# Side steps of a hybrid decoder trunk: a pause ahead of three-matrix groups, additions one step at a time at a shorter period, and one product for the values of the first 128 keys

## The chip, the cores and the metric

The kernel runs on one core of one Trainium2 chip. The metric is the device time of that core in microseconds, the median of three runs. The core has a matrix engine (PE, with its weight loads shown as PEld), a vector engine (DVE), a scalar engine (ACT), a general engine (POOL) that here mostly issues transfers, and a queue (SP) that issues the other transfers. Each engine and each queue runs its own instructions in a fixed order and waits where one of them needs something that is not there yet.

## The reference

A trunk of two layers over 256 positions of width 2048, in 32-bit floats:

```python
for layer in range(DEPTH):                      # DEPTH = 2
    mix = even_mixer(h, ...) if layer % 2 == 0 else odd_mixer(h, ...)
    h = layer_norm(ALPHA * h + mix, ...)
    h = layer_norm(ALPHA * h + conv_ffn(h, ...), ...)

def conv_ffn(x, w_up, conv_w, conv_b, w_down):
    a, u = jnp.split(x @ w_up, 2, axis=-1)      # 2048 -> 2 x 5632
    a = causal_depthwise_conv(a, conv_w, conv_b)
    return (jax.nn.silu(a) * u) @ w_down        # 5632 -> 2048
```

The even mixer holds a state-space scan (16 heads) and a softmax attention (8 heads); the odd mixer holds an attention with three branches (compressed keys, selected keys, window; 8 heads) and a retention (8 heads). At 256 positions every key is in reach, so an attention head is causal attention over two tiles of 128 keys: the first 128 queries see the first 128 keys, the second 128 queries see all 256.

## The kernel before

**Numbers in two parts.** A 32-bit product is made of three products of shorter numbers: ACT rounds a block of weights to its high part (`whi`, line 210), DVE subtracts to get the low part (`wlo`, line 218), and PE multiplies high by high, low by high and high by low. A block (a slab) is 128 x 1024 numbers, 512 KB. SP loads slabs into six buffers `wraw`; there are four buffers each of `whi` and `wlo`. `Weights.get(i)` (line 258) prepares slabs up to `i + 3` before the products of slab `i` are written down.

**Ordinary groups.** `group_b` (387) computes 256 columns over 16 tiles of 128 rows: 4 slabs of 4 tiles, products in line 427. With its last tile it writes the evacuation of the group (`ev_a` with the convolution, lines 1667 to 1684, or `ev_u`, 1686 to 1694), which runs on ACT and DVE. After every second tile it takes one step from each of two queues of side work, `self.fill` and `self.aux`. So such a group has eight places for a step; the last one stands behind the evacuation. The first group of an up phase, of three column blocks, has 15 places.

**Wide groups and kept sums.** `group_m` (517) computes 1024 columns and saves products in some pairs of row tiles: seven small products of sums of blocks replace eight. Plans name pairs: `P` plain, `N` with weight sums made on the spot by DVE (`add_up`, 224, four additions into the tile `other` or `sums`), `R` with weight sums made earlier and kept in memory. Up phases hold wide groups at j = 7 in layer 0 and at j = 4, 8 and 12 in layer 1 (`WIDE_UP`, line 36), all with the plan `NPNPNPNP`. A wide group of an up phase takes its side steps from `aux` alone (line 525: `fill = self.aux if inner else self.fill`); `self.fill` stands still in it.

**Side work of an up phase.** `Weights.make` (231) gives three steps for a kept sum: `load` (POOL brings four blocks into `sums`, two transfers of 512 KB, line 240), `add` (DVE, four additions of 128 x 512 in one step, line 246, each depending on the one before) and `store` (POOL writes the result back, two transfers, line 250). All of them are pinned: they stay behind whatever was written earlier for their engine. `cycles` (483) lays these steps into `self.fill` with empty steps between them, `period` steps for a sum. With one buffer the next load cannot start until the store has landed. Layer 0 makes six sums with two buffers at period 10 and then 15 with one at period 13; layer 1 makes 15 with one buffer at period 14 (`CYCLES`, line 38). The even layer makes two at period 20. Behind each wide group six empty steps are put at the head of `self.fill` (line 1725).

`residual` (863) lays its steps into `aux`: four loads of two rows into the tile `room` (POOL, line 869, pinned), and behind each of them two pairs of vector instructions, `gain` (873, pinned) and `bias` (877). The POOL queue thus carries loads and stores of sums and these row loads in the order of the steps.

**Other places.** `sum_up` (499) makes sums of activations for the pairs with seven products: five vector instructions and a split. `attn_steps` (1086) gives three steps for a head; the last, `mix` (1148), multiplies the softmax weights by the values, in full 32-bit products: three in the even layer, eight in the odd one, all 128 columns wide.

Instructions are ordered within an engine by a planner that keeps pinned ones in place and otherwise takes what it believes ready first.

## Time and profile before

| what | value |
|---|---|
| median of three runs | 2248.83 us (2248.74 to 2249.03) |
| span of the profiled execution | 2246.8 us |
| PE busy | 2235.3 us, 99% of the span |
| PEld busy | 1920.9 us, 85% |
| DVE busy | 1831.3 us, 82% |
| ACT busy | 1254.0 us, 56% |
| POOL busy | 126.4 us, 6% |
| mean granted clock | 0.999 |
| transfers | 546.33 MB, 243 GB/s in the mean |

The page gives the span of the profiled execution, from its first to its last instruction, and no other time for it; the median of the runs is 2.03 us above that span, which is what lies around it. A row of a timeline gives start, length, engine, line, operation, what is written from what, shape, the number of instructions merged into the row, and in brackets the idle time before it with what ended it. A matmul's length is modelled, and successive ones overlap; the distance from start to start is what one costs. A product of full 32-bit numbers shows as two records.

### The profile page before, as it was taken

What the parts mean: (1) busy time and instruction counts of PE and PEld (TensorE: products, weight loads), DVE (VectorE), ACT (ScalarE), POOL (GpSimd) and SP (SyncE); (2) the same over time, 40 slices, a digit from 0 to 9 for tenths busy, and PEclk for the clock granted to TensorE, in tenths of its full rate; (3) what the DMA queues carried; (4) which work ended last, traced back from release to release, by engine and by line L of the source; (5) the groups of instructions that cost most, each with busy time, mean ns of one, the idle gap of its engine ahead of it and who ended that gap; (6) DMA issues with size and microseconds to landing.
All of it is one profiled execution on the core that took longest, in us unless ns stands there. A gap on an engine that the chain in (4) does not pass through costs nothing.

```text
span 2246.8 us, 32995 instructions
## 1 busy us (share of the span) xinstructions
PE 2235.3 (99%) x12125; PEld 1920.9 (85%) x12125; DVE 1831.3 (82%) x2795; ACT 1254.0 (56%) x1718; POOL 126.4 (6%) x219
## 2 busy tenths in 40 slices
PE   9999999999999999999999999999999999999998
PEld 9888888888888888888898888888888888888887
DVE  5788688988877778887977777889988887779887
ACT  5555555655555556656645564457555565557563
POOL 0101000110011100000000000000100001100000
PEclk9999999999999999999999999999999999999999
DMA  9854456897788886888668534467876768888884
GB/s 312 292 175 161 158 194 189 274 376 264 238 302 302 296 284 213 292 286 274 211 208 287 188 114 154 152 209 235 290 227 228 255 217 297 300 273 276 276 280 169
DMA packets 158780, 546.33 MB, mean 243 GB/s; under 512 B 17827, under 2 KB 19283, under 8 KB 158483
## 3 DMA queue, kind: packets, MB, share of 16 engines
q1 hardware_dynamic: 132937, 451.41, 60.1%
q0 software_dynamic: 25536, 92.55, 11.8%
q8 instruction: 95, 1.56, 0.3%
q14 instruction: 68, 0.56, 0.1%
q10 hardware_dynamic: 144, 0.26, 0.0%
HBM read 502.19 MB, written 41.96 MB: 242 GB/s over the span
## 4 chain that ended last, share of the span: by engine, by line
PE 96%; DVE 2%; issue 1%; ACT 0%; POOL 0%; DMA 0%; SPq 0%; ACTq 0%; POOLq 0%; DVEq 0%
PE acc L427 51%; PE ps L540 7%; PE ps L541 7%; PE ps L539 7%; PE acc L627 3%; PE acc L629 3%; PE acc L628 3%; PE acc L540 3%; PE acc L541 3%; PE acc L539 3%; PE ps L628 1%; PE ps L627 1%; PE ps L629 1%; PE ps L1161 1%; PE ps L427 1%
## 5 line engine op out<-in xcount | busy, mean ns | idle before, releaser
L210 ACT ACTIVATE whi<-wraw 128x1024 fp32r<-128x1024 f32 (+4 forms) x882 | 875.1, 1002 | 549.6 <-PE acc L427 219.0
L218 DVE TENSOR_TENSOR wlo<-wraw,whi 128x1024 fp32r<-128x1024 f32 (+4 forms) x882 | 1007.5, 1153 | 209.6 <-ACT whi L210 197.6
L427 PE MATMUL acc<-x,whi 128*128 128x512 f32 x3296 | 1032.2, 398 | 0.0
L427 PEld LDWEIGHTS acc<-x,wlo 128*128 128x128 f32 x3296 | 604.0, 188 | 136.5 <-DVE wlo L218 0.3
L427 PE MATMUL acc<-x,wlo 128*128 128x256 f32 x3296 | 633.8, 279 | 0.0
L427 PEld LDWEIGHTS acc<-x,whi 128*128 128x128 f32 x3296 | 510.0, 189 | 9.7 <-issue 1.1
L689 ACT ACTIVATE tmp<-acc 128x512 f32<-128x512 f32 x104 | 62.2, 598 | 167.8 <-PE acc L427 167.7
L246 DVE TENSOR_TENSOR sums<-sums 128x512 f32<-128x512 f32 x140 | 96.2, 687 | 10.5 <-DMA sums<-in_down 9.4
L540 PE MATMUL ps<-wlo,g 128*128 128x512 f32 x260 | 101.3, 390 | 0.0
L541 PE MATMUL ps<-whi,g 128*128 128x512 f32 x260 | 101.2, 389 | 0.0
L539 PE MATMUL ps<-whi,g 128*128 128x512 f32 x260 | 101.2, 389 | 0.0
L539 PE MATMUL ps<-whi,x 128*128 128x512 f32 x244 | 94.0, 390 | 2.7 <-ACT whi L210 2.7
L540 PE MATMUL ps<-wlo,x 128*128 128x512 f32 x244 | 95.5, 391 | 0.1
L541 PE MATMUL ps<-whi,x 128*128 128x512 f32 x244 | 95.0, 389 | 0.0
L627 PE MATMUL acc<-whi,x 128*128 128x344 f32 (+3 forms) x224 | 74.9, 336 | 0.7 <-ACT whi L210 0.7
L628 PE MATMUL acc<-wlo,x 128*128 128x344 f32 (+3 forms) x224 | 74.5, 333 | 0.3 <-DVE wlo L218 0.3
L629 PE MATMUL acc<-whi,x 128*128 128x344 f32 (+3 forms) x224 | 74.3, 332 | 0.0
L1681 DVE SCALAR_TENSOR_TENSOR c<-fpad,prm,c 128x256 f32<-128x256 f32 x176 | 74.2, 479 | 0.0
L210 ACT ACTIVATE whi<-other 128x1024 fp32r<-128x1024 f32 x32 | 33.7, 1055 | 57.7 <-DVE other L229 56.9
L250 POOL DMA_DIRECT2D sumdown<-sums x62 | 33.3, 537 | 570.9 <-DVE sums L246 570.8
L540 PEld LDWEIGHTS ps<-wlo,g 128*128 128x128 f32 x260 | 48.8, 188 | 10.5 <-DVE wlo L218 0.4
L539 PEld LDWEIGHTS ps<-whi,g 128*128 128x128 f32 x260 | 48.8, 188 | 10.3
(458 smaller groups left out, 3141.6 us busy)
## 6 DMA issues: line engine op xcount, KB each, us to landing
wraw<-in_up SPq DMA_DIRECT2D x328, 512.0 KB, 4.8
wraw<-in_down SPq DMA_DIRECT2D x142, 512.0 KB, 4.8
wraw<-in_od_in SPq DMA_DIRECT2D x96, 512.0 KB, 4.2
wraw<-in_ev_in SPq DMA_DIRECT2D x72, 512.0 KB, 4.1
wraw<-sumdown SPq DMA_DIRECT2D x68, 512.0 KB, 4.5
sums<-in_down POOLq DMA_DIRECT2D x62, 512.0 KB, 6.8
sumdown<-sums POOLq DMA_DIRECT2D x62, 512.0 KB, 5.4
wraw<-in_ev_out SPq DMA_DIRECT2D x30, 512.0 KB, 3.9
```

What stands on the lines that cost most here:

```text
L210: a = nc.scalar.activation(hi[:, :n], raw[:, :n], AF.Copy)
L218: b = nc.vector.tensor_tensor(lo[:, :n], raw[:, :n], hi[:, :n].bitcast(F32), op=OP.subtract)
L246: self.tc.keep_in_program_order(nc.vector.tensor_tensor(o, x, y, op=OP.add))
L427: nc.tensor.matmul(acc, wt, mv, start=(k == 0 and i < len(unit)), stop=(k == nk - 1 and i >= len(unit)))
L539: nc.tensor.matmul(o, xh, wh, start=n not in used, stop=False)
L540: nc.tensor.matmul(o, xh, wl, start=False, stop=False)
L541: nc.tensor.matmul(o, xl, wh, start=False, stop=stop)
L627: nc.tensor.matmul(o, xh, wh, start=start, stop=False)
L628: nc.tensor.matmul(o, xh, wl, start=False, stop=False)
L629: nc.tensor.matmul(o, xl, wh, start=False, stop=stop)
L689: nc.scalar.activation(t, a[:, :, 256:], AF.Copy, scale=sign)
L1681: nc.vector.scalar_tensor_tensor(c[:, i, :], pad[:, i, t:t + 256], w[:, t:t + 1], c[:, i, :], op0=OP.mult, op1=OP.add)
```

## The change

1. `add` becomes three steps. The first adds two pairs of blocks in one instruction of 128 x 1024 (`first` from `first` and `both`, which are the first two blocks, and the second and fourth); the other two are 128 x 512 as before. It needs both loaded halves at once. Each step of the list is taken at its own place.
2. `cycles` is laid out anew. With one buffer: load, five empty steps, three additions, store, `period - 10` empty steps, next load. With two: three additions, store, `period - 6` empty steps, load, one empty step.
3. The period of layer 1 goes from 14 to 12.
4. Ahead of the last ordinary group before a wide one, eight empty steps are put at the head of `self.fill`.
5. `sum_up` does two of its subtractions in one instruction, 128 x 256 in place of two of 128 x 128.
6. `mix` multiplies the values of the first 128 keys for all 256 queries in one product, and likewise the compressed branch: two products in the even layer, five in the odd one.

```diff
-CYCLES = ((6, 10, 13), (0, 0, 14))
+CYCLES = ((6, 10, 13), (0, 0, 12))
...
-        def add():
-            for o, x, y in ((b11, b11, b12), (b12, b12, b22), (b22, b11, b22), (b21, b22, b21)):
-                self.tc.keep_in_program_order(nc.vector.tensor_tensor(o, x, y, op=OP.add))
+        first, both = s[:, 0:1024].rearrange("p (i c) -> p i c", i=2), s.rearrange("p (i c) -> p i c", i=4)[:, 1:4:2, :]
+
+        def add(o, x, y):
+            return lambda: self.tc.keep_in_program_order(nc.vector.tensor_tensor(o, x, y, op=OP.add))
+
+        adds = [add(*a) for a in ((first, first, both), (b22, b11, b22), (b21, b22, b21))]
...
-    def cycles(self, keys, bufs, period):
-
-        fill, made = self.fill, [self.w.make(k, self.dram, bufs[i % len(bufs)]) for i, k in enumerate(keys)]
-        n, wait = len(bufs), min(5, period - 4)
+    def cycles(self, keys, bufs, period, fill=None):
+
+        fill, made = fill or self.fill, [self.w.make(k, self.dram, bufs[i % len(bufs)]) for i, k in enumerate(keys)]
+        n = len(bufs)
         fill.add(made[0][0])
-        if n == 1:
-            fill.add(period - 4 - wait)
-        else:
+        if n == 2:
             fill.add(3, made[1][0], 6)
-        for i, (_, add, store) in enumerate(made):
-            fill.add(add, 1, store)
+        for i, (_, adds, store) in enumerate(made):
+            if n == 1:
+                fill.add(5)
+            fill.add(*adds, store)
+            if i + 1 < len(made):
+                fill.add(period - (10 if n == 1 else 6))
             if i + n < len(made):
-                fill.add(wait, made[i + n][0])
-            if i + 1 < len(made):
-                fill.add(period - 4 - wait)
+                fill.add(made[i + n][0])
+            if n == 2:
+                fill.add(1)
...
-        a11, a21, a12, a22 = v[:, 0, :128], v[:, 0, 128:], v[:, 1, :128], v[:, 1, 128:]
-        s1, s2, s4, s3 = (u[:, 128 * i:128 * i + 128] for i in range(4, 8))
-        for o, p, q in ((s1, a21, a22), (s2, a11, s1), (s4, a12, s2), (s3, a21, a11)):
+        a11, a21, a12 = v[:, 0, :128], v[:, 0, 128:], v[:, 1, :128]
+        s3, s1, s2, s4 = (u[:, 128 * i:128 * i + 128] for i in range(4, 8))
+        ends = u[:, 0:512].rearrange("p (i t) -> p i t", i=4)[:, 0:4:3, :]
+        for o, p, q in ((u[:, 512:768].rearrange("p (i t) -> p i t", i=2), a21[:, None, :].to_broadcast([128, 2, 128]), ends),
+                        (s2, a11, s1), (s4, a12, s2)):
             nc.vector.tensor_tensor(o, p, q, op=OP.subtract)
-        self.split(hi, lo, u[:, 512:896])
+        self.split(hi, lo, u[:, 640:1024])
...
-            for t in range(2):
-                mms = []
-                for b, (_, _, v) in enumerate(branches):
-                    pt = st["pt"][b]
-                    if t == 0:
-                        mms.append((v(0), pt[:, 0:128]))
-                    else:
-                        mms += [(v(0), pt[:, 128:256]), (v(1), pt[:, 256:384])]
-                if cmp:
-                    mms.append((cmp[0], cmp[1][:, t * 128:(t + 1) * 128]))
-                for i, (a, b) in enumerate(mms):
-                    nc.tensor.matmul(o[:, t * 128:(t + 1) * 128], a, b, start=(i == 0), stop=(i == len(mms) - 1))
+            mms = [(v(0), pt[:, 0:256], 0) for (_, _, v), pt in zip(branches, st["pt"])]
+            mms[1:1] = [(v(1), pt[:, 256:384], 128) for (_, _, v), pt in zip(branches, st["pt"])]
+            if cmp:
+                mms[1:1] = [(cmp[0], cmp[1], 0)]
+            for i, (a, b, c) in enumerate(mms):
+                nc.tensor.matmul(o[:, c:256], a, b, start=(i == 0), stop=(i == len(mms) - 1))
...
                 elif j not in wide and j - 1 not in wide:
+                    if j + 1 in wide and i % 2:
+                        self.fill.q[:0] = [lambda: None] * 8
                     self.group_b(x, [e])
```

## The prediction

> **What bounds the kernel now.** I read the page's engine shares and its chain first, then the chain in order of time, then timelines of the places where it leaves PE.

> ```profile
> span 2246.8 us, 32995 instructions
> PE 2235.3 (99%) x12125; PEld 1920.9 (85%) x12125; DVE 1831.3 (82%) x2795; ACT 1254.0 (56%) x1718; POOL 126.4 (6%) x219
> PE 96%; DVE 2%; issue 1%; ACT 0%; POOL 0%; DMA 0%; SPq 0%; ACTq 0%; POOLq 0%; DVEq 0%
> ```

> PE sets the time. Work on DVE or POOL is worth nothing unless PE waits for it, and 2246.8 - 2235.3 = 11.5 us is all that PE stands idle. The change can win where a wait for DVE ends on PE, or by fewer PE cycles; it can lose where it makes DVE late by more than DVE's lead. The four wide groups of the up phases show the first. The rows are the first product of each (j = 7, then 4, 8, 12) from the timeline, and the piece of the chain that begins behind each.

> ```profile
> 528.39 0.39 PE L539 MATMUL ps<-whi,x 128*128 128x512 f32 x1
> 571.15 8.36 PE acc L427 x48
> 1611.06 0.39 PE L539 MATMUL ps<-whi,x 128*128 128x512 f32 x1
> 1654.14 8.36 PE acc L427 x48
> 1700.41 0.39 PE L539 MATMUL ps<-whi,x 128*128 128x512 f32 x1
> 1741.83 8.36 PE acc L427 x48
> 1788.10 0.39 PE L539 MATMUL ps<-whi,x 128*128 128x512 f32 x1
> 1829.52 8.36 PE acc L427 x48
> ```

> The same work takes 42.76, 43.08, 41.42 and 41.42 us: two groups lose 1.34 and 1.66 us against the other two. Around the loss at j = 7 stand these rows of DVE, ACT and PE:

> ```profile
> 532.29 0.69 DVE L246 TENSOR_TENSOR sums<-sums 128x512 f32<-128x512 f32 x1
> 536.97 0.69 DVE L246 TENSOR_TENSOR sums<-sums 128x512 f32<-128x512 f32 x1
> 538.77 0.69 DVE L229 TENSOR_TENSOR other<-other,wraw 128x512 f32<-128x512 f32 x1
> 539.58 1.06 ACT L210 ACTIVATE whi<-other 128x1024 fp32r<-128x1024 f32 x1 [6.08 <-DVE other L229]
> 539.08 0.39 PE L539 MATMUL ps<-whi,part 128*128 128x512 f32 x1
> 540.69 0.50 PE L539 MATMUL ps<-whi,x 128*128 128x512 f32 x1 [1.22 <-ACT whi L210]
> ```

> Four additions of a kept sum (the first and last are shown) run between the evacuation and the weight sums of line 229, ACT waits 6.08 us for those, PE for ACT. In the list of steps these additions have the last place ahead of the group, behind the evacuation. At j = 4 it is the same; at j = 8 and 12 the additions lie elsewhere.

> **The change part by part.**

> *Pause.* The eight empty steps fill the last ordinary group, and the wide group takes none from this list, so the additions leave both places. In DVE's stream of j = 4 the rows below show an addition and the next instruction 0.60 us apart: 4 x 0.60 = 2.4 us leave the queue ahead of line 229, more than either loss. j = 7 then becomes like j = 8: **-1.34 us** (0 to -1.34). The additions go to ordinary groups, where DVE has room (below).

> *j = 4 is not so simple*, because the order on POOL's queue changes there. I replayed the two lists of layer 1 by hand, counting places from 1, 15 of them in the first group and 8 in each other. Before: second sum added at 41, stored at 43, the last two rows of `room` loaded at 46, third sum loaded at 49, added at 55, the last place before j = 4. After: additions at 39, 40, 41, store 42, load of the third sum 45, rows 46. So the row loads now stand behind a load of a sum that must wait until the store has landed.

> ```profile
> 1597.84 0.54 POOL L250 DMA_DIRECT2D sumdown<-sums  x1 [1.95 <-DVE sums L246]
> 1599.58 0.55 POOL L869 DMA_DIRECT2D room<-in_lnrow  x1 [1.20 <-DVE r L873]
> 1603.74 0.53 POOL L240 DMA_DIRECT2D sums<-in_down  x1 [1.34 <-DMA sumdown<-sums]
> DMA to landing us min/median/max: 4.6/7.0/8.6
> 1607.80 0.69 DVE L873 SCALAR_TENSOR_TENSOR r<-r,room 128x512 f32<-128x512 f32 x1
> 1619.70 0.69 DVE L246 TENSOR_TENSOR sums<-sums 128x512 f32<-128x512 f32 x1
> 1620.30 0.69 DVE L229 TENSOR_TENSOR other<-other,wraw 128x512 f32<-128x512 f32 x1
> DVE r L873 <- DMA room<-in_lnrow: 3.4, 1, 3.4
> ```

> (The fourth row is the landing of `room`, the last one the only wait for it, in layer 0.) Before, the row load goes out at 1599.58 and lands about 7.0 later at 1606.6, just ahead of its use at 1607.80. After, the store goes out between 1595.3 (three additions in a row from where the first stood) and 1597.8, lets the load behind it go 5.9 later (1597.84 to 1603.74), and then, 0.53 later, the row load at 1601.7 to 1604.3; landing 1608.7 to 1611.3. DVE stops at line 873, pinned, for 0.9 to 3.5 us, and queued behind it are low parts, the evacuation and line 229. Net with the 2.4 us gone: the loss of 1.66 shrinks by 1.5 in the one case and grows by 1.1 in the other. I take the middle, a wait of 2.2 us that eats nearly all of the 2.4, since the third addition is written one slab behind the first: **-0.2 us** (-1.66 to +1.1).

> *Shorter period, additions as steps.* Pace and chain in layer 1 behind the last wide group:

> ```profile
> 1672.64 27.94 PE acc L427 x160
> 1849.89 140.29 PE acc L427 x804
> 1848.00:1990.00 142.00, 142.00 (x815) 123.95 (x814) 108.72 (x139) 74.22 (x91) 16.59 (x31) 1.00 0.85 297
> 1867.54 1.67 DVE L1681 SCALAR_TENSOR_TENSOR c<-fpad,prm,c 128x256 f32<-128x256 f32 x4
> 1869.13 0.69 DVE L246 TENSOR_TENSOR sums<-sums 128x512 f32<-128x512 f32 x1
> 1869.73 1.22 DVE L218 TENSOR_TENSOR wlo<-wraw,whi 128x1024 fp32r<-128x1024 f32 x1
> 1874.58 0.54 POOL L250 DMA_DIRECT2D sumdown<-sums  x1 [2.20 <-DVE sums L246]
> 1880.07 0.53 POOL L240 DMA_DIRECT2D sums<-in_down  x1 [1.66 <-DMA sumdown<-sums]
> 1886.98 1.42 DVE L246 TENSOR_TENSOR sums<-sums 128x512 f32<-128x512 f32 x2 [2.67 <-DMA sums<-in_down]
> ```

> (The third row lists PE, PEld, DVE, ACT and POOL busy, then the clock, the share of transfers and GB/s.) A step is 8 of the chain's products, 27.94 / 20 = 1.40 us; 14 steps are 19.6 us, 12 are 16.8. DVE is busy for 108.72 of 142 us, so the work fits. But a sum is also a loop through memory: store out to load out 5.49 us (1874.58 to 1880.07), load out to data 6.91 (to 1886.98, where DVE waited for it): 12.4 us, and 0.5 from addition to store. The additions themselves: 1.2 (a 128x1024 as in line 218), 0.6, 0.6, and one slab's low part, 1.2, between them: 3.6 us when they stand at the second, third and fourth place of a group; when they stand at the sixth, seventh and eighth, the third is behind an evacuation (line 1681 and more), about 2 us longer, 5.6. By my replay the two kinds alternate. Two loops: 16.5 + 18.5 = 35.0 us against 24 steps, 33.6. So the loop is **longer than its period** by 1.4 us in two sums, 10 sums lie behind j = 12, and DVE falls back 4.5 x 1.4 = 6.3 us, waiting at the first addition with the low parts behind it. What covers it is DVE's lead: at least 2.7 us (the wait of 2.67 lies inside the unbroken chain piece from 1849.89), at most three slabs, 8.4; the middle is 5.5. So 6.3 - 5.5 = **+0.8 us**, with ends of nothing (cover of 8.4) and 6.3 - 2.7 = 3.6; every 1 us on each loop would be 9 more (below).

> Layer 0 with period 13 has 18.2 us against a mean loop of 17.5, and keeps its cover; period 10 with two buffers has 28 us a buffer. In the even layer the additions come nearer to their load by six steps; a wait there is covered as the one below is, inside a piece of the chain without a break. Without that cover it would be some 2 us.

> ```profile
> 62.40 0.69 DVE L1196 TENSOR_SCALAR r<-r 128x1024 f32<-128x1024 f32 x1 [3.77 <-DMA r<-in_xt]
> 53.10 79.57 PE acc L427 x456
> ```

> *Values in one product.* Two records of 128 columns, and two of 256 (line 1593):

> ```profile
> 1284.88 0.39 PE L1161 MATMUL ps<-pt,vs 128*128 128x128 f32 x2
> 1285.10 0.39 PE L1161 MATMUL ps<-pt,vw 128*128 128x128 f32 x2
> 1361.64 0.60 PE L1593 MATMUL ps<-q,k 128*128 128x256 f32 x2
> 1362.07 0.39 PE L1594 MATMUL ps<-q,k 128*128 128x128 f32 x2
> ```

> 0.22 us against 0.43: cost goes by columns, and two products joined save 0.01 us. Three joins in each of 8 odd heads, one in each of 8 even ones: 32 x 0.01 = **-0.3 us** (0 to -0.5 with rounding of the rows).

> *Fewer instructions in additions and `sum_up`*: some tenths of a us of DVE each, 0 on PE: DVE's spare time, 33 of 142 us above, hides them.

> **Sum:** -1.34 - 0.2 + 0.8 - 0.3 = -1.0 us; span 2246.8 to 2245.8. The runs' median, 2248.83, is 2.03 above the span, and I keep that: **2247.8 us**.

> **Rivals.** A change of 0.2% or 4.5 us is about what can be told from none.

> *Both wide groups heal.* If the row loads land before 1608, j = 4 gives its 1.66 too, and if the loop stays within its cover: -1.34 - 1.66 - 0.3, 2245.5. For it speaks the early end above (0.9 us of wait); against it, that rows land late behind sums. [...]

> *The loop decides: slower.* Place: layer 1 from j = 12 on. If shorter distances between sums raise traffic (GB/s is 297 there already) and each loop takes 1.2 us more, DVE falls back by 3.8 us in two sums, 17.1 in all; 17.1 - 5.5 = 11.6 us show on PE, and with the -1.8 of the rest that is 2258.6. It passes 0.2% at 6.3 us on PE, which is 0.6 us more in each loop. For it: the wait of 2.67 at period 14 already. Against: a late DVE is itself a longer interval, and the 2.67 was caught up.

> *The pause does not do it.* DVE's low parts alone hold PE up at j = 7 as before: 0.8 - 0.3, 2249.3. Against it stand j = 8 and 12, which have all but the additions.

> *Products cost by the record.* 64 records less at 0.11 us: -7.0 in place of -0.3, 2241.1. The rows of line 1593 speak against it.

> **How the numbers follow.** Forecast 0.45 (its own range 2245.7 to 2251.9, from the ends at j = 4 and of the loop); both heal 0.25; the loop 0.17; no effect of the pause 0.09; by the record 0.04. Faster by over 0.2% (below 2244.3): the last and a fifth of the second, 0.09. Slower (above 2253.3): two thirds of the loop's and a little of the forecast's, 0.14. The range 2244.4 to 2254.5 leaves out the record case and the loop's upper half.

> **What would show it.** j = 7: first product to the next group's in 41.4 us, no addition of line 246 from the evacuation on. j = 4: row loads on POOL behind line 240; a wait of DVE at line 873 for `room`, and still 42.5 us or more. Layer 1 at the end: waits of DVE on `sums` of 2 to 5 us at nearly every first addition, and the chain leaving PE or not. Line 1161: 112 records in place of 176. It is wrong if the chain breaks anywhere else, or if the planner moves other work.

## The result, and the profile after

The changed kernel takes **2263.87 us** (median of 5 runs, 2262.90 to 2267.22) against 2248.83 in the same session (5 runs, 2248.55 to 2251.11): a ratio of 1.0068, with a 95% interval of 1.0056 to 1.0081. It is slower by 15 us, and the prediction of 2247.8 (2244.4 to 2254.5) was wrong. The profiled execution has a span of 2262.1 us, 15.3 more than before.

The page's first part and its chain, as they stand now:

```profile
span 2262.1 us, 32785 instructions
PE 2240.5 (99%) x12061; PEld 1920.7 (85%) x12061; DVE 1822.5 (81%) x2717; ACT 1252.4 (55%) x1718; POOL 124.5 (6%) x219
PE 90%; DMA 5%; DVE 2%; issue 2%; POOL 0%; ACT 0%; SPq 0%; DVEq 0%; POOLq 0%; ACTq 0%
```

The chain, which was 96% PE and 0% DMA, now goes over transfers for 5% of the span. Idle time of PE has grown from 11.5 us to 2262.1 - 2240.5 = 21.6. Of the 5 us by which PE is busy longer, 3.4 are two stretches of 3.41 us at a granted clock of 0.50 (below).

Where the time came from is read from the starts of the wide groups. A wide group is measured here from its first product to the first product of the next group (0.16 us less than in the prediction, where the mark was the next piece of the chain), and the end stretch from the first product at j = 12 to the last product of the program. The ten experiments below are in the same table. The stretches are those of one profiled execution for each kernel, the medians those of 5 or 11 runs; for experiments 7 and 9 the profiled execution was faster than the median (2256.66 and 2249.37 us). "Ratio" is to runs of the kernel before from the same session as each, with its 95% interval.

| kernel | j = 7 | j = 4 | j = 12 to the end | median | ratio |
|---|---|---|---|---|---|
| before | 42.60 | 42.92 | 453.31 | 2248.83 | |
| changed | 41.25 | 46.95 | 466.05 | 2263.87 | 1.0068 (1.0056 to 1.0081) |
| 1 period 14 | 41.26 | 43.78 | 453.37 | 2247.70 | 0.9994 (0.9985 to 1.0003) |
| 2 additions together | 41.26 | 48.62 | 453.34 | 2252.76 | 1.0015 (1.0006 to 1.0023) |
| 3 rows first | 41.32 | 42.07 | 467.77 | 2259.53 | 1.0045 (1.0032 to 1.0058) |
| 4 period 13 | 41.30 | 43.26 | 455.59 | 2248.74 | 0.9999 (0.9991 to 1.0008) |
| 5 late, together | 41.25 | 41.24 | 455.43 | 2246.34 | 0.9988 (0.9980 to 0.9997) |
| 6 late, spread | 41.26 | 41.32 | 471.87 | 2264.29 | 1.0061 (1.0048 to 1.0074) |
| 7 no pause in layer 1 | 41.26 | 46.64 | 459.85 | 2258.63 | 1.0040 (1.0028 to 1.0053) |
| 8 two parts alone | 41.29 | 43.30 | 453.37 | 2247.20 | 0.9992 (0.9983 to 1.0001) |
| 9 late by 51 | 41.25 | 41.24 | 458.31 | 2253.30 | 1.0017 (1.0006 to 1.0028) |
| 10 late, period 13 | 41.26 | 43.14 | 455.16 | 2248.01 | 0.9996 (0.9987 to 1.0005) |

So the change gained 1.35 us at j = 7, lost 4.03 at j = 4, another 0.8 at j = 8, and lost 12.7 from j = 12 on. The loss at j = 8 is in none of the ten experiments (41.25 to 41.33 us there), and its cause stays open.

**The end of layer 1.** The waits of DVE in the stretch from 1850 to 2100 us, of the kernel before and of the changed one (us in all, times, longest):

```profile
DVE sums L246 <- DMA sums<-in_down: 3.5, 3, 2.7
```

```profile
DVE sums L247 <- DMA sums<-in_down: 50.2, 9, 7.7
```

One turn of the loop, in the changed kernel's timelines of DVE and POOL (the additions are line 247 now, stores 253):

```profile
1885.70 1.23 DVE L247 TENSOR_TENSOR sums<-sums 128x1024 f32<-128x1024 f32 x1 [3.45 <-DMA sums<-in_down]
1886.85 1.22 DVE L218 TENSOR_TENSOR wlo<-wraw,whi 128x1024 fp32r<-128x1024 f32 x1
1887.98 0.68 DVE L247 TENSOR_TENSOR sums<-sums 128x512 f32<-128x512 f32 x1
1888.58 1.22 DVE L218 TENSOR_TENSOR wlo<-wraw,whi 128x1024 fp32r<-128x1024 f32 x1
1889.72 0.68 DVE L247 TENSOR_TENSOR sums<-sums 128x512 f32<-128x512 f32 x1
...
1903.93 1.23 DVE L247 TENSOR_TENSOR sums<-sums 128x1024 f32<-128x1024 f32 x1 [6.20 <-DMA sums<-in_down]
```

```profile
1890.96 0.54 POOL L253 DMA_DIRECT2D sumdown<-sums  x1 [3.20 <-DVE sums L247]
1891.49 0.53 POOL L240 DMA_DIRECT2D sums<-in_down  x1
1896.82 0.54 POOL L240 DMA_DIRECT2D sums<-in_down  x1 [4.79 <-DMA sumdown<-sums]
```

The chain of waits for the same turn, and the one behind it (start, us, what):

```profile
1890.96 5.57 DMA sumdown<-sums
...
1896.82 7.01 DMA sums<-in_down
...
1910.85 5.61 DMA sumdown<-sums
...
1916.75 6.10 DMA sums<-in_down
```

The turn from 1885.70 to 1903.93 takes 18.23 us: 4.70 from the start of the first addition to the end of the third (1890.40), 0.56 to the store, 5.86 to the load, 7.01 until it has landed, 0.10 to the next addition. The one behind it, to 1922.87, takes 18.94 (third addition's end at 1910.56, behind an evacuation; store at 1910.85, load at 1916.75). Twelve steps are 16.8. The first additions of the last ten sums start from 1849.11 to 2015.86, nine turns of 18.53 us in the mean, while the products ask for one every 16.8. PE meets it in the low parts queued behind the waiting addition; one stop of six such in its timeline:

```profile
1925.29 0.50 PE L430 MATMUL acc<-x,wlo 128*128 128x256 f32 x2 [1.68 <-DVE wlo L218]
```

**j = 4.** POOL, DVE and PE of the changed kernel, from their timelines:

```profile
1600.19 0.54 POOL L240 DMA_DIRECT2D sums<-in_down  x1 [2.86 <-DMA sumdown<-sums]
1600.73 1.08 POOL L876 DMA_DIRECT2D room<-in_lnrow  x2
```

```profile
1591.80 1.23 DVE L247 TENSOR_TENSOR sums<-sums 128x1024 f32<-128x1024 f32 x1 [1.42 <-DMA sums<-in_down]
...
1610.03 0.69 DVE L880 SCALAR_TENSOR_TENSOR r<-r,room 128x512 f32<-128x512 f32 x1 [3.13 <-DMA room<-in_lnrow]
```

```profile
1611.91 0.50 PE L547 MATMUL ps<-wlo,x 128*128 128x512 f32 x1 [1.43 <-DVE wlo L218]
...
1616.79 0.67 PE L547 MATMUL acc<-wlo,part 128*128 128x512 f32 x1 [1.30 <-DVE wlo L218]
1617.26 0.63 PE L548 MATMUL acc<-whi,part 128*128 128x512 f32 x1
1617.68 0.63 PE L546 MATMUL acc<-whi,part 128*128 128x512 f32 x1
```

```profile
1600.73 9.28 DMA room<-in_lnrow
```

The last row is from the chain of waits. The row loads stand behind the second load of the third sum, go out at 1600.73 and land 9.3 later; DVE stands still for 3.13 us at the gain step, and PE stops several times. From 1616.95 on a product of 512 columns costs 0.43 us from start to start, where it is 0.23 from 1620.54 on: the granted clock is 0.50 for 3.41 us.

### The profile page after: what moved, and what is told of

Its sections match the earlier page's. It is cut to its first block, busy times and chain, and to the rows that moved or that the text cites. A ratio compares the mean times of both kernels' runs of the same rounds, so it can differ in the third digit from the quotient of the medians.

```text
span 2262.1 us, 32785 instructions
## 1 busy us (share of the span) xinstructions
PE 2240.5 (99%) x12061; PEld 1920.7 (85%) x12061; DVE 1822.5 (81%) x2717; ACT 1252.4 (55%) x1718; POOL 124.5 (6%) x219
## 4 chain that ended last, share of the span: by engine, by line
PE 90%; DMA 5%; DVE 2%; issue 2%; POOL 0%; ACT 0%; SPq 0%; DVEq 0%; POOLq 0%; ACTq 0%
PE acc L430 44%; PE ps L547 7%; PE ps L546 7%; PE ps L548 7%; PE acc L634 3%; PE acc L635 3%; PE acc L636 3%; PE acc L547 3%; PE acc L548 3%; PE acc L546 3%; DMA sums<-in_down 2%; DMA sumdown<-sums 2%; PE ps L636 1%; PE ps L635 1%; PE ps L634 1%
## 5 line engine op out<-in xcount | busy, mean ns | idle before, releaser
L210 ACT ACTIVATE whi<-wraw 128x1024 fp32r<-128x1024 f32 (+4 forms) x882 | 874.2, 1001 | 521.9 <-PE acc L430 198.6
L218 DVE TENSOR_TENSOR wlo<-wraw,whi 128x1024 fp32r<-128x1024 f32 (+4 forms) x882 | 1005.2, 1151 | 179.0 <-ACT whi L210 167.6
L430 PEld LDWEIGHTS acc<-x,wlo 128*128 128x128 f32 x3296 | 604.0, 188 | 148.4 <-DVE wlo L218 12.7
L247 DVE TENSOR_TENSOR sums<-sums 128x512 f32<-128x512 f32 (+1 forms) x105 | 90.6, 863 | 75.3 <-DMA sums<-in_down 68.5
L1679 ACT ACTIVATE c<-fpad,prm 128x256 f32<-128x256 f32 x88 | 47.9, 592 | 39.9 <-DVE fpad L699 39.7
L210 ACT ACTIVATE whi<-other 128x1024 fp32r<-128x1024 f32 x32 | 33.7, 1055 | 55.3 <-DVE other L229 53.1
```

Of the source, the lines that this page charges most:

```text
L210: a = nc.scalar.activation(hi[:, :n], raw[:, :n], AF.Copy)
L218: b = nc.vector.tensor_tensor(lo[:, :n], raw[:, :n], hi[:, :n].bitcast(F32), op=OP.subtract)
L247: return lambda: self.tc.keep_in_program_order(nc.vector.tensor_tensor(o, x, y, op=OP.add))
L430: nc.tensor.matmul(acc, wt, mv, start=(k == 0 and i < len(unit)), stop=(k == nk - 1 and i >= len(unit)))
```

## The experiments

The first theory: the one-buffer loop of layer 1 takes about 18.5 us and the period of 12 steps gives it 16.8, which costs the end; and at j = 4 the order on POOL is to blame. Rivals: the additions as three steps disturb DVE whatever the period, the pauses do it by pushing sums into the end, or DVE has no slack ahead of j = 4 for whatever reason.

**1. Period 14.** All else as changed, the pause in layer 0 alone.

```diff
-CYCLES = ((6, 10, 13), (0, 0, 12))
+CYCLES = ((6, 10, 13), (0, 0, 14))
...
-                    if j + 1 in wide and i % 2:
+                    if j + 1 in wide and i % 2 and not layer:
```

> Layer 1 back to a period of 14 steps, and the pause kept only in layer 0 (with 14 steps a sum there is no room for it in layer 1); all else as changed. Theory (the kept sums of layer 1 are a loop through memory that takes about 18.5 us, which 12 steps of 1.40 us cannot hold and 14 steps, 19.6 us, can): the 12.8 us that the last stretch of layer 1 lost come back, less than 1.5 us of them stay, the stretch around j = 4 is within 1 us of before, and with -1.8 from j = 7 and the values the time is 2247 (2246 to 2248.5). Rival (the additions as three steps, one of them twice as wide, disturb DVE whatever the period): 5 us or more of the last stretch stay, 2252 or more.

2247.70 us; the end stretch is back at 453.37. DVE's waits in it, from 1850 to 2100 us:

```profile
DVE sums L247 <- DMA sums<-in_down: 6.9, 3, 3.2
```

The rival falls: three steps at the old period cost the end nothing.

**2. Additions together.** Period 12 and the pauses stay. The edit holds for every sum with one buffer, so those of layer 0 change too (here and in experiments 5, 9 and 10).

```diff
-            fill.add(*adds, store)
+            fill.add(*([lambda adds=adds: [a() for a in adds], store, 2] if n == 1 else [*adds, store]))
```

> The changed kernel, with the three additions of a kept sum in one step, the store in the next one and two empty steps behind it (one buffer); period 12 and the pauses kept. Theory (what makes the loop long is that the additions are spread over three steps, up to 6 us from first to third, because low parts and an evacuation stand between them): first to third addition takes about 2 us, the loop gets 2 to 4 us shorter, 14.5 to 16.5 us, and fits 16.8; at least 8 us of the 12.8 come back, 2251 to 2256. Rival (the loop is made of the waits for landing, 12.4 us and more, and those grow when the sums follow closer): less than 4 us come back, 2260 to 2264.

2252.76 us: the end stretch is back entirely, though the period is 12. The rival falls. The expected size was off: the planner still puts low parts between the three, so they take 3.7 or 4.7 us in turn and not 2. The two kinds, from DVE's timeline:

```profile
1899.76 1.95 DVE L247 TENSOR_TENSOR sums<-sums 128x1024 f32<-128x1024 f32 x2 [1.25 <-DMA sums<-in_down]
1901.63 1.22 DVE L218 TENSOR_TENSOR wlo<-wraw,whi 128x1024 fp32r<-128x1024 f32 x1
1902.77 0.68 DVE L247 TENSOR_TENSOR sums<-sums 128x512 f32<-128x512 f32 x1
...
1917.43 1.22 DVE L247 TENSOR_TENSOR sums<-sums 128x1024 f32<-128x1024 f32 x1
1918.56 1.22 DVE L218 TENSOR_TENSOR wlo<-wraw,whi 128x1024 fp32r<-128x1024 f32 x1
1919.70 0.68 DVE L247 TENSOR_TENSOR sums<-sums 128x512 f32<-128x512 f32 x1
1920.30 1.22 DVE L218 TENSOR_TENSOR wlo<-wraw,whi 128x1024 fp32r<-128x1024 f32 x1
1921.44 0.68 DVE L247 TENSOR_TENSOR sums<-sums 128x512 f32<-128x512 f32 x1
```

The loop comes down to 16.96 us in the mean, hardly more than 16.8. The third addition behind an evacuation, which made it 6.6 to 6.9 us, is what is gone. At j = 4 this kernel is the worst of all, 48.62: its row loads go out at 1604.22, 3.5 later than in the changed kernel.

**3. Rows first.** In layer 1 the queue `aux` runs two places earlier, so that the last row loads stand ahead of the load of the third sum.

```diff
-    def residual(self, idx, tiles, fill=None, sums=()):
+    def residual(self, idx, tiles, fill=None, sums=(), ahead=18):
...
-        fill.add(18)
+        fill.add(ahead)
...
-                self.residual(2 * layer, [[room[:, 0:512], room[:, 512:1024]]] * 4, self.aux, sums)
+                self.residual(2 * layer, [[room[:, 0:512], room[:, 512:1024]]] * 4, self.aux, sums, 16 if layer else 18)
```

> The changed kernel, with the steps of the row loads in layer 1 (queue aux) two places earlier, so that the last two rows of room are issued on POOL ahead of the load of the third sum; nothing else moved in the list of sums. Theory (the stop at j = 4 comes from the row loads standing behind a load that waits for a store): DVE no longer waits at the gain step, the TensorE clock stays at 1.0 there, and the wide group j = 4 takes 41.4 to 41.8 us from its first product to the next group's; 4.5 to 5.7 us less than the changed kernel, 2258 to 2259.5, the last stretch as before. Rival (DVE is late there for the added work of the sums itself): j = 4 still takes 44 us or more, 2261 to 2264.

2259.53 us, near the expectation; the wait for `room` and the low clock there are gone (the products of 512 columns behind 1616.86 are 0.23 us apart), and j = 4 falls from 46.95 to 42.07. The vector steps of `aux` run two places earlier with the loads, so this does not test the order on POOL quite alone. Two things were not as expected: 0.8 us of loss stays at j = 4, and the end stretch grew from 466.05 to 467.77, with two stretches at half clock, from 1921.91 (3.41 us at 0.50) and 1997.01 us, where the changed kernel has one (1.7 us each).

**4. Period 13**, with a pause only ahead of j = 7 and j = 4.

```diff
-CYCLES = ((6, 10, 13), (0, 0, 12))
+CYCLES = ((6, 10, 13), (0, 0, 13))
...
-                    if j + 1 in wide and i % 2:
+                    if j + 1 in (4, 7) and i % 2:
```

> Layer 1 with a period of 13 steps, 18.2 us, and a pause only ahead of j = 7 and j = 4; all else as changed. Here the last two row loads stand one place ahead of the load of the third sum. Theory: the loop of 18.5 us is 0.3 us longer than the period, over some 8 sums 2.4 us, less than the lead of DVE: the last stretch loses 0 to 2 us, j = 4 takes 41.4 us (-1.7 against before), together 2245.3 to 2247.5. Rival (any period below 14 makes DVE wait in earnest, since the waits feed on themselves): the last stretch loses 5 us or more, 2250 to 2254.

2248.74 us, above the expected range. The end stretch loses 2.28, which leaves the rival out. But j = 4 takes 43.26, although here the row loads are ahead of the sum, DVE does not wait for them, and no addition stands at the last place. The stop is a new one (PE's timeline):

```profile
1613.99 0.50 PE L547 MATMUL acc<-wlo,part 128*128 128x512 f32 x1 [1.30 <-DVE wlo L218]
```

It waits for a low part on DVE, which in this kernel (with a wait for a sum ahead of it) and in the one before stands in these rows:

```profile
1592.22 1.23 DVE L247 TENSOR_TENSOR sums<-sums 128x1024 f32<-128x1024 f32 x1 [2.04 <-DMA sums<-in_down]
...
1612.72 1.22 DVE L218 TENSOR_TENSOR wlo<-other,whi 128x1024 fp32r<-128x1024 f32 x1
```

```profile
1613.28 1.22 DVE L218 TENSOR_TENSOR wlo<-other,whi 128x1024 fp32r<-128x1024 f32 x1
```

Before, it ended at 1614.50 and was in time, since PE came to j = 4 at 1611.06; now it ends at 1613.94 and is late, since PE comes at 1608.53. Of the 2.5 us that PE has won by then, DVE has won 0.6. That gave the second theory: ahead of j = 4 DVE has no slack, by its work before and by its work and its waits for sums now, and gains of PE are given back there; the order on POOL is one part of it only. The windows from 1580 to 1612 us show the work (length, then PE, PEld and DVE busy): 31.04 of 32 us on DVE in the kernel before, and 28.36 in the next experiment, which leaves the sums out of this stretch. The busy time alone does not tell a late DVE, though: this kernel has 28.80 us there and experiment 10 has 28.53, hardly more, and both lose j = 4. They also wait about 2 us at a pinned addition (2.04 and 1.90), with the work behind it still to do.

```profile
1580.00:1612.00 32.00, 32.00 (x185) 27.88 (x184) 31.04 (x47) 16.18 (x21) 5.38 (x10) 1.00 0.99 353
```

```profile
1580.00:1612.00 32.00, 32.00 (x181) 27.77 (x180) 28.36 (x38) 17.05 (x21) 3.20 (x6) 1.00 0.74 239
```

**5. Late start, additions together.** No pause in layer 1; its sums begin so late that none is added or stored ahead of j = 4; only the first load is issued there, with the last step but one.

```diff
-                self.fill.add(20)
+                self.fill.add(53 if layer else 20)
```

(beside the edits of experiment 2 and the second of experiment 1)

> The changed kernel with the three additions in one step (as in the second experiment), no pause in layer 1, and 53 empty steps in place of 20 ahead of layer 1's sums, so that no sum is loaded, added or stored before the wide group j = 4; period 12. Theory (ahead of j = 4 DVE has no slack, 70.7 us of work in 72 before the change, and the two sums made there, some 5 us of additions, are what makes the low parts late): j = 4 takes 41.3 to 41.6 us, the clock stays at 1.0, the last stretch is as before; with -1.35 at j = 7 and -0.6 from the values the time is 2245.3 (2244.5 to 2246.3), faster than both kernels. Rival (the row steps of the residual alone make DVE late there): j = 4 stays at 42.5 us or more, 2246.5 to 2248.

2246.34 us, just above the expected range, and faster than both kernels: ratio 0.9988, 0.9980 to 0.9997. j = 4 takes 41.24 us. DVE now waits for its input ahead of the group, and the low part that was late in experiment 4 ends at 1611.50:

```profile
1608.94 0.69 DVE L699 TENSOR_TENSOR u<-acc,tmp 128x512 f32<-128x512 f32 x1 [1.88 <-ACT tmp L696]
1609.67 0.69 DVE L1692 TENSOR_TENSOR u<-u,c 128x512 f32<-128x512 f32 x1
1610.28 1.22 DVE L218 TENSOR_TENSOR wlo<-other,whi 128x1024 fp32r<-128x1024 f32 x1
```

The row steps are all still there, so they are not enough to make DVE late; with them, the sums are. The end stretch stays 2.1 us longer than before. (Experiment 10 shows where.)

**6. The same with the additions as three steps.**

```diff
-            fill.add(*([lambda adds=adds: [a() for a in adds], store, 2] if n == 1 else [*adds, store]))
+            fill.add(*adds, store)
```

> The kernel of the experiment before with one thing put back: the additions are three steps again (first at the same place). Theory (the spread additions alone make the loop 18.5 us long, whatever happens at j = 4): j = 4 as in that kernel, and the stretch from j = 12 to the end 10 to 15 us longer than in it; 2256 to 2260. Rival (the loss at the end was inherited from the late DVE at j = 4 or from the pauses): less than 4 us longer, under 2250.

2264.29 us, above the expected range. j = 4 is as good as in experiment 5 (41.32), and the end stretch is 16.4 us longer, more than expected: turns of 18.75 us, one stretch at half clock (from 2012.47 us; the mean clock is 0.998, and 1.0 in experiment 5), and a stop of 2.46 us in the down phase, whose start is late too. Nothing is inherited from j = 4. The additions take 3.7 us in every other turn here, although DVE waits up to 8 us just ahead of them:

```profile
1932.41 1.95 DVE L247 TENSOR_TENSOR sums<-sums 128x1024 f32<-128x1024 f32 x2 [8.12 <-DMA sums<-in_down]
1934.28 1.22 DVE L218 TENSOR_TENSOR wlo<-wraw,whi 128x1024 fp32r<-128x1024 f32 x1
1935.41 0.68 DVE L247 TENSOR_TENSOR sums<-sums 128x512 f32<-128x512 f32 x1
```

In the other turns, with the evacuation behind the first of the three, they mostly take 6.6 or 6.9.

**7. No pause in layer 1**, all else as changed (the second edit of experiment 1 alone).

> The changed kernel without the pauses of layer 1 (kept in layer 0); period 12, additions as three steps. Eight sums instead of ten are then left behind j = 12, and three lie ahead of j = 4. Theory (each sum behind j = 12 costs the difference of loop and period, 18.5 - 16.8 = 1.7 us, once DVE's lead of about 3 us is used): the last stretch loses 8 x 1.7 - 3 = 10.6 us (8 to 12) against 12.8, and j = 4, with more additions ahead of it, is no better than 44 us; 2259 to 2264. Rival (the pauses themselves cost the time, by pushing the sums into the end): the last stretch loses less than 6 us, 2255 or less.

2258.63 us. The end stretch loses 6.5, between theory (8 to 12) and rival (less than 6). The price of a sum was right, the count was not: eight sums make seven turns, of 18.33 us here, so 7 x 1.53 = 10.7, and DVE's lead is more than the 3 us taken. For the changed kernel the same account gives 9 x 1.73 = 15.6 us of falling back; it lost 12.7, of which 1.7 are a half-clock stretch, so the lead covered 15.6 - 11.0 = 4.6. With that lead, 10.7 - 4.6 = 6.1 us are due here, and 6.5 were lost. The lead is an estimate, and how half-clock stretches count in it is not shown: in experiment 3, nine turns of 18.74 us and 13.2 us lost ahead of the down phase give 7.7 with its two stretches taken off and 4.3 without, where the changed kernel gives 4.6 and 2.8. The pauses thus do cost, and by this account through the two sums that they move behind j = 12.

**8. Two parts alone:** the kernel before with the pause ahead of j = 7 and the values in one product (the change's edit of `mix`, and the one below).

```diff
+                    if j + 1 in wide and i % 2 and not layer:
+                        self.fill.q[:0] = [lambda: None] * 8
```

> The kernel before with only two parts of the change: the pause ahead of j = 7 (layer 0) and the values in one product. Theory (these two parts gained what the traces of the changed kernel show, -1.35 and about -0.6 us, and nothing else of the change is needed for it): j = 7 takes 41.3 us, the sum is 2246.9 (2246.2 to 2247.8). Rival (the gain at j = 7 needs the additions as steps of their own, or the gain of the two is given back at j = 4, where DVE is full): j = 4 longer than 43.5 us, 2248 to 2249.

2247.20 us, as the theory had it; the interval of the ratio, 0.9983 to 1.0001, still holds 1. j = 7 takes 41.29 with the additions in one step as before. j = 4 is 43.30, within the theory's 43.5, 0.4 longer than before.

**9. The start at 51 in place of 53.**

```diff
-                self.fill.add(53 if layer else 20)
+                self.fill.add(51 if layer else 20)
```

> The kernel of the fifth experiment (late start, additions in one step) with 51 empty steps in place of 53: each addition two places earlier in its group, at the first and fifth place behind j = 12 as in the second experiment, the last store two places ahead of the end. Theory (the 2.1 us that the last stretch still lost there come from the last sums ending at the very last place, so that the down phase starts with late weights and x): the last stretch is 453.4 us as before the change, and the time 2244.3 (2243.6 to 2245.6). Rival (the loss there is the order in which the start of the down phase is taken, and has nothing to do with the sums' place): the last stretch stays 2 us longer, 2246 to 2247.

A miss: 2253.30 us. The end stretch is 458.31, worse than in experiment 5. An addition now stands at the last place but one ahead of j = 12, and the wide group there stops as j = 4 did:

```profile
1789.05 0.50 PE L547 MATMUL acc<-wlo,part 128*128 128x512 f32 x1 [1.30 <-DVE wlo L218]
```

That is 1.8 of the 5.0 us; the other 3.2 are lost in the down phase. The loop is 17.03 us, and the eleven runs lie between 2246.8 and 2261.6; those of experiment 2, with a loop of 16.96 in the same period, lie within 2.8 us. What spreads the runs here is not shown.

**10. Late start at period 13:** the edits of experiments 2 and 3, no pause in layer 1, period 13, and

```diff
-                self.fill.add(20)
+                self.fill.add(38 if layer else 20)
```

> Additions in one step as in the second experiment, row loads of layer 1 two places earlier as in the third, no pause in layer 1, 38 empty steps ahead of its sums (one sum lies ahead of j = 4, nine places before it) and a period of 13. Theory (a loop of about 16 us in a period of 18.2 has 2 us of slack, so that late landings no longer reach DVE; and one sum nine places ahead of j = 4 still leaves DVE room): j = 4 takes 41.3 to 41.8 us, the last stretch 453.4 us, the time 2244.5 (2243.8 to 2245.8), and the runs lie within about 2 us of each other, where those of the fifth experiment spread over 3.6 us and those of the ninth over 14.8. Rival (the last stretch loses its 2 us for another reason than the sums, or the one sum already makes DVE late at j = 4): 2246 to 2248.

2248.01 us, the rival. One sum, added nine places ahead of j = 4, is enough to lose it (43.14), with the row loads in time: DVE waits 1.90 us for that sum.

```profile
1596.60 1.22 DVE L247 TENSOR_TENSOR sums<-sums 128x1024 f32<-128x1024 f32 x1 [1.90 <-DMA sums<-in_down]
```

The end stretch still loses 1.85 us. In experiments 5 and 10 DVE waits 1.8 us at the start of the down phase for the last store to land, before `sums` is used for something else; the waits of DVE, ACT and PE from 2010 to 2060 us in this kernel hold the line

```profile
DVE sums L920 <- DMA sumdown<-sums: 1.8, 1, 1.8
```

and the kernel before has no such wait. That this makes the 2 us was not tried. Where they are lost can be read, however, from the first product of the down phase, here in the kernel before and in experiment 5:

```profile
2009.79 0.39 PE L539 MATMUL ps<-whi,g 128*128 128x512 f32 x1
```

```profile
2005.19 0.39 PE L546 MATMUL ps<-whi,g 128*128 128x512 f32 x1
```

From the start of j = 12 to it both take 221.69 us, and so do experiments 4 and 10; the changed kernel takes 234.45. So in experiments 4, 5 and 10 PE loses nothing to the loop behind j = 12, and their 1.9 to 2.3 us are all lost in the down phase.

## Why the prediction was wrong, and where it was right

**Wrong: the loop of layer 1 (+0.8 us forecast, +12.7 measured).** The mechanism and the place were in the prediction; the term was mis-sized, and its rival "the loop decides" (2258.6, chance 0.17) was the case. Two turns were put at 35.0 us and are 37.1. Of the first kind's 18.23 us against 16.5 forecast, 1.1 are the additions: I let one low part stand between the three (3.6 us), and there are two (4.7). The second kind has 6.6 to 6.9 for 5.6. The waits for landing were 0.4 and 0.1 us longer in the first turn, and 0.4 longer and 0.8 shorter in the second, so the rival's own reason, more traffic, was not what made it true. Nor does a late DVE by itself lengthen the additions: experiment 1 has them at 4.7 us in four sums for which DVE waits for nothing, and experiment 6 at 3.7 behind long waits. Why the planner puts one low part between them or two stays open; where they lie in the order is the likely reason. The prediction's "a late DVE is itself a longer interval, and the 2.67 was caught up" failed too: the waits at the first additions grew from 3.05 us (1866.90) to between 5.2 and 7.7 (from 1903.93 on). The deficit is then 9 x 1.73 = 15.6 us in place of 6.3. The cover of 5.5, the middle of a wide range, was near the 4.6 worked out above, and the rest of the 12.7 is the half-clock stretch of 1.7. Experiments 1, 2 and 6 show from three sides that the length of the turn against the period is the cause: a longer period, or closer additions at the same period, bring all of the loss back, and spreading them again costs 16.4.

**Wrong: j = 4 (-0.2 forecast, +4.0 measured).** The order on POOL and the wait at the gain step were as described. The row loads went out at 1600.73, earlier than the forecast's earliest (1601.7), but landed 9.3 us later instead of 7.0, so that the wait was 3.13 and not 2.2. Missing in the step were three things: the new first addition needs both loaded halves and waited 1.42 us itself (1591.80); PE came 2.3 us earlier, and DVE did not; and the stops brought a stretch at half clock, 3.41 us at half speed, 1.7 us. "At j = 4 it is the same" as at j = 7 was the wrong reading: the row steps stand there too, DVE had no slack, and without the additions at the last place a low part is late instead (experiments 3, 4 and 10). Experiment 5 shows that with the sums out of this stretch j = 4 takes 41.24; whether their additions or their waits matter more was not tried apart.

**Right: the pause at j = 7.** 42.60 to 41.25, the forecast -1.34; experiment 8 shows it without the rest of the change.

**Right at the odd layer's heads: the values.** Records fell from 176 to 112. The start of the heads moved from 1.97 us ahead of the kernel before (first pair) to 2.17 (last pair), so 0.2 us were gained there, where 24 x 0.01 was forecast. Before j = 7 the changed kernel is 0.47 ahead, and 0.79 if counted from the first product behind the start (6.06 in place of 5.74 us), where the even layer's share was put at under 0.1. Most of that is not the values: experiment 8, which has them and of the rest the pause alone, is 0.20 ahead by the same count. What else of the change moved it was not tried apart.

**Layer 0 at period 13 "keeps its cover":** true in the changed kernel, but barely. DVE waits 16.9 us there, six times; in experiments 1 and 6, which have the same layer 0, it was over 41 us, eleven times, and PE stopped once at 720 us, for 0.7 and 1.0 us. What differs between these executions was not followed up.

**Additions and `sum_up` with fewer instructions:** nothing on PE, as forecast. "The pause does not do it" and "by the record" were rightly held unlikely; "both heal" failed at j = 4.

## What to carry to other kernels

Where side work goes through one buffer and memory, add up its whole turn, with the work that the order puts between its steps: here about 1 us more of that in each turn made most of the loss. Once the period is shorter than the turn, every turn costs the difference as soon as the lead is used up. Keep the steps of such a turn together, or its period above the turn. And a microsecond won on the bounding engine is kept only if the next place downstream has slack on the engine that feeds it: look there for that engine's work and its waits before adding up gains, since its busy share alone did not tell the kernels that lost j = 4 from the one that did not.

## What the runs showed of the hardware

In the profiled execution of the changed kernel the granted clock is 0.50 in three stretches, each behind stops of PE: for 3.41 us from 1616.95 and from 2019.72 us, and from 2258.66 us, behind the last product, to the end of the span. The starts are 402.77 and 238.94 us apart, which is 118 and 70 times 3.413. In each trace I laid a grid of 3.413 us through the start of a half-clock stretch. The rows give PE's busy time of one such stretch as the second number behind the times, and the clock as the third from the end; the first three are of the changed kernel at j = 4, the last three of experiment 6.

```profile
1610.12:1613.53 3.41, 1.98 (x8) 1.05 (x6) 3.41 (x5) 1.30 (x2) 0.00 (x0) 1.00 0.03 12
1613.53:1616.95 3.42, 1.41 (x5) 0.65 (x5) 3.39 (x6) 1.32 (x2) 0.00 (x0) 1.00 0.50 153
1616.95:1620.36 3.41, 3.41 (x9) 2.65 (x10) 3.41 (x5) 1.21 (x2) 0.00 (x0) 0.50 0.21 35
```

```profile
1930.56:1933.97 3.41, 1.56 (x9) 1.03 (x7) 1.53 (x2) 0.00 (x0) 0.00 (x0) 1.00 0.02 10
1933.97:1937.38 3.41, 1.83 (x11) 1.65 (x12) 3.41 (x5) 0.00 (x0) 1.07 (x2) 1.00 0.56 180
1937.38:1940.80 3.42, 3.42 (x22) 2.98 (x21) 3.42 (x7) 2.26 (x4) 0.53 (x1) 1.00 1.02 373
```
